# Level products of a chunk: column groups of the array in turn, head by head

## Chip, cores and metric

The kernel runs on one NeuronCore of a Trainium2 chip. The metric is the device time of one execution in microseconds (us): the median over runs. TensorE is PE, with its weight loads shown apart as PEld, VectorE is DVE, ScalarE ACT, GpSimdE POOL; SyncE (SP) issues the transfers.

## What is computed

One layer of a hybrid decoder for a prompt of 1024 tokens and a sample group of 64 tokens: a SwiGLU block, a mixing block, a second SwiGLU block. The mixing block has a windowed attention and, beside it, a gated linear recurrence (HGRN2) with four heads of 128 keys and 128 values. The change touches the recurrence alone. Within a chunk its reference is

```python
G = jnp.cumsum(gb, axis=2)                       # gb = log f
diff = G[:, :, :, None, :] - G[:, :, None, :, :]
decay = jnp.exp(jnp.where(causal, diff, -jnp.inf))
A = jnp.einsum('bhtk,bhsk,bhtsk->bhts', qb, kb, decay)
o = jnp.einsum('bhts,bhsv->bhtv', A, vb) + jnp.einsum('bhtk,bhkv->bhtv', qb * jnp.exp(G), S)
```

with queries `qb`, keys `kb` = 1 - f, and f the forget gate, all float32. `A[t, s]` is a product of a query and a key over 128 key channels, each channel decayed by the gates between s and t.

## The kernel before

**Tokens and stages.** Tokens are worked on in three chunks, n = 0, 1, 2. Chunk 0 has 320 columns (256 prompt tokens and the 64 sample tokens), chunks 1 and 2 have 384 (`WIDTH`, line 26). In blocks of 128 tokens that is two for chunk 0 and three each for the others (`NPB`). The activations lie transposed: channels on the partitions, tokens along the free dimension. For each chunk the combined projection (`w_in_units`, line 1096) makes z; from it come the gates `f`, the queries `Q` and the keys `K`, each a tile of 128 x 4 x width, the 4 being the heads.

**The level products.** `intra` (line 1258) builds A for all blocks of a chunk. It doesn't form the decays pair by pair: it goes through levels h = 1, 2, 4, ..., 64. At level h the tokens are split into pieces of 2h; for a query in the second half of a piece and a key in its first half, the decay is that of the query since the middle times that of the key up to the middle. After each level Q's second halves and K's first halves are multiplied by the gate products `D` of that level (lines 1324 on DVE and 1326 on POOL), so at the next level they hold the decay over a longer stretch. The next level's products need both.

For h up to 16 one call of `blocks` (line 1270) makes all products of a level: for every 32 tokens, number i, and every head a, a matmul with 32 columns of K as the stationary operand and the same 32 columns of Q as the moving one. The result, 32 x 32, goes to PSUM partitions 32 (i mod 4) to 32 (i mod 4) + 31, at a place along the free dimension given by j = i // 4 and a. An operand's columns decide which 32 columns of the array hold it: a product for partitions 0 to 31 uses column group 0, one for 32 to 63 group 1, and so on; all products use all 128 rows. `blocks` is called once as "ld" for the diagonal (line 1290, masked by L1293) and then for each level as "lv" (line 1302); DVE picks the entries of the level by a mask into `C` (line 1305). Each call for chunk 0 makes 10 x 4 products at the diagonal and h = 1, 2, 4, and 8 x 4 at h = 8, 16, where the sample tokens are left out; each call for chunks 1 and 2 makes 12 x 4. Such a run of products is called a burst below.

For h = 32 and 64 the products are written out in `intra` (lines 1308 to 1316, tile "l"): at h = 32 with 32 columns for partitions 0 to 31 and 64 to 95, at h = 64 with 64 columns for partitions 0 to 63. ACT copies them to A (line 1320).

A float32 product shows in the trace as two records of a weight load and two of a matmul.

**What sets the order.** `intra` is a generator that yields after each level. The main program walks through the large projections and calls `tick` (line 127) every few matmuls; `tick` calls `pace` (line 108), which steps the generators of the queue "hg" so that a chunk is done by its due time (`DUE`). The levels of chunk 0 so lie between matmuls of the projection and of the first SwiGLU block's second product (line 283 to 285, `mm3`: three passes of split operands for one product), those of chunks 1 and 2 between the projections of the following work. A scheduler that works with a model of time then fixes the order on each engine; engines work in order.

**Around it.** `load_w` and `split` (lines 259 to 271) bring weights: a transfer to `raw`, a rounded copy `wsph` or `w` on ACT (line 260), the rest on DVE (line 261). The activations of the first SwiGLU block come back from memory as `ar` (line 971). In the attention, line 1242 ("pv") makes its products in pairs for partitions 0 to 63 and 64 to 127; in the attention of the sample group, line 1451 ("spv") makes four products for the four groups of 32 partitions in turn.

Of the kernel before, what the change touches and what calls it, by code (L numbers as in the profile page):

```python
# [18 lines left out]
P = 128  # L19
# [24 lines left out]
def tile_step(ctx: ExitStack, tc: tile.TileContext, A: dict, O: list):  # L44
# [10 lines left out]
    def uid(s):  # L55
        cnt[0] += 1
        return f"{s}_{cnt[0]}"
# [4 lines left out]
    def axbank(s="ax"):  # L62
        return ps.tile([P, 512], F32, tag="ax", bufs=4, name=uid(s))
# [984 lines left out]
    def mixing(tp, h):  # L1048
# [209 lines left out]
        def intra(n):  # L1258

            z, w, wp = Z[n], WIDTH[n], P * NPB[n]  # L1260
            f, Q = z["f"][:, :, :w], z["hq"][:, :, :w]
            K = tp.tile([P, 4, 384], F32, tag="K", name=uid("K"))[:, :, :w]
            D = tp.tile([P, 1524], F32, tag="D", name=uid("D"))
            C = tp.tile([P, 3, 4, 32], F32, tag="cm", name=uid("cm"))
            parts = [(slice(0, P), slice(0, NPB[n]))] + ([(slice(0, NS), slice(2, 3))] if n == 0 else [])

            def span(h):
                return w if h <= 4 else wp

            def blocks(s, x, y, h):  # L1270
                b4 = axbank(s)[:, :384].rearrange("p (j a t) -> p j a t", j=3, a=4)
                for i in range(span(h) // 32):
                    j, cs, ps_ = i // 4, slice(32 * i, 32 * i + 32), slice(32 * (i % 4), 32 * (i % 4) + 32)
                    for a in range(4):
                        PE.matmul(b4[ps_, j, a], x[:, a, cs], y[:, a, cs], start=True, stop=True)  # L1275
                return b4

            def flat(t, rs, js):
                return t[rs, js].rearrange("p j a t -> p (j a) t")

            S.activation(K, f, AF.Copy, bias=1.0, scale=-1.0)
            Ds, off, h = [f], 0, 1
            while h <= 64:
                nx = span(h) // (2 * h)
                Dv = Ds[-1][:, :, :2 * nx].rearrange("p a (x e) -> p a x e", e=2)
                Ds.append(D[:, off:off + 4 * nx].rearrange("p (a x) -> p a x", a=4))
                G.tensor_tensor(Ds[-1], Dv[:, :, :, 0], Dv[:, :, :, 1], op=ALU.mult)
                off += 4 * nx
                h *= 2
            b4 = blocks("ld", K, Q, 1)  # L1290
            for rs, js in parts:
                c = flat(C, rs, js)
                V.tensor_tensor(c, flat(b4, rs, js),  # L1293
                                ident32[rs].unsqueeze(1).to_broadcast([c.shape[0], c.shape[1], 32]), op=ALU.mult)
            V.tensor_tensor(Q, Q, f, op=ALU.mult)
            yield
            At = z["f"]
            h = 1
            while h <= 64:
                ws = span(h)  # L1300
                if h <= 16:
                    b4 = blocks("lv", K, Q, h)
                    for rs, js in parts[:2 if h <= 4 else 1]:
                        c = flat(C, rs, js)
                        V.copy_predicated(c, lmask[h][rs].unsqueeze(1).to_broadcast([c.shape[0], c.shape[1], 32]),
                                          flat(b4, rs, js))
                else:
                    for j0 in range(0, NPB[n], 64 // h + 1):
                        js = range(j0, min(NPB[n], j0 + 64 // h + 1))
                        b4 = axbank(f"l{h}")[:, :len(js) * 4 * h].rearrange("p (j a t) -> p j a t", j=len(js), a=4)  # L1310
                        for j in js:
                            for c in range(0, P, 2 * h):
                                for a in range(4):
                                    k0 = j * P + c
                                    PE.matmul(b4[c:c + h, j - j0, a], K[:, a, k0:k0 + h], Q[:, a, k0 + h:k0 + 2 * h],
                                              start=True, stop=True)
                        Av = At[:, :, P * j0:P * j0 + P * len(js)].rearrange("p a (j t) -> p j a t", j=len(js))
                        for c in range(0, P, 2 * h):
                            for j in range(len(js)):
                                S.copy(Av[c:c + h, j, :, c + h:c + 2 * h], b4[c:c + h, j])  # L1320
                nx = ws // (2 * h)
                Qv, Kv = [t[:, :, :ws].rearrange("p a (x u) -> p a x u", u=2 * h) for t in (Q, K)]
                Dv = Ds.pop(0)[:, :, :2 * nx].rearrange("p a (x e) -> p a x e", e=2)
                V.tensor_tensor(Qv[:, :, :, h:], Qv[:, :, :, h:], Dv[:, :, :, 0:1].to_broadcast([P, 4, nx, h]),
                                op=ALU.mult)
                G.tensor_tensor(Kv[:, :, :, :h], Kv[:, :, :, :h], Dv[:, :, :, 1:2].to_broadcast([P, 4, nx, h]),
                                op=ALU.mult)
                if h == 1:
                    G.memset(At[:, :, :w], 0.0)
                if h == 4 and n == 0:  # L1330
                    z["Ds"] = Ds[0]
                if h == 16:
                    for i in range(4):
                        r, nj = slice(32 * i, 32 * i + 32), 3 if n == 0 and i < 2 else NPB[n]
                        Av = At[r, :, :384].rearrange("p a (j t) -> p j a t", j=3)
                        for j in range(nj):
                            G.tensor_copy(Av[:, j, :, r], C[r, j])
                h *= 2
                yield
            z["K"], z["D"] = K, Ds[0]  # L1340
# [186 lines left out]
        def ready(kind, n):  # L1527
            if n not in MT:
                MT[n] = new_h(n)
            if kind == "at":  # L1530
                gens = [(attn_block(n, b), 9) for b in range(NPB[n])]
                if n == 0:
                    gens += [(sample_attn(), 17), (kv_out(0), 1)]
                if n == 2:
                    gens.append((kv_out(2), 1))
            else:
                gens = [(intra(n), 8)] + [(hgrn_block(n, b), 3) for b in range(NPB[n])]
                if n == 0:
                    gens.append((sample_hgrn(), 14))
                if n == 2:  # L1540
                    gens.append((state_out(), 1))
            queues[kind] += [[n, g, left] for g, left in gens]
# [59 lines left out]
    h = {}  # L1602
# [195 lines left out]
```

## Time and profile before

| | |
|---|---|
| median of 3 runs | 1988.52 us (1987.66 to 1989.71) |
| the profiled execution's own time | 1992.03 us |
| its span, first to last instruction | 1990.3 us |
| granted TensorE clock, mean | 0.998 |
| matmul records | 13549 |
| moved by DMA | 359.54 MB, mean 181 GB/s |

The profile is that of one execution, 3.5 us above the median of the runs. Its views give: the busy time of each engine, whole or in windows ("724.00:790.00 66.00, 66.00 (x786) ..." is a stretch, its length, then busy time and instructions of each engine); groups of instructions by line; and a timeline in which a row is the start, the length, the engine, the line, and out<-in with the shape and the count of like instructions in sequence. "128*32 128x32" is a matmul that uses 128 rows and 32 columns of the array and has a moving operand of 128 x 32. A matmul's own length holds its way through the array, so matmuls in a row overlap; what counts is the time from start to start.

### The profile page before, as it was taken

What the parts mean: (1) busy time and instruction counts of PE and PEld (TensorE: products, weight loads), DVE (VectorE), ACT (ScalarE), POOL (GpSimd) and SP (SyncE); (2) the same over time, 40 slices, a digit from 0 to 9 for tenths busy, and PEclk for the clock granted to TensorE, in tenths of its full rate; (3) what the DMA queues carried; (4) which work ended last, traced back from release to release, by engine and by line L of the source; (5) the groups of instructions that cost most, each with busy time, mean ns of one, the idle gap of its engine ahead of it and who ended that gap; (6) DMA issues with size and microseconds to landing.
All of it is one profiled execution on the core that took longest, in us unless ns stands there. A gap on an engine that the chain in (4) does not pass through costs nothing.

```text
span 1990.3 us, 34623 instructions
## 1 busy us (share of the span) xinstructions
PE 1972.9 (99%) x13549; PEld 1854.7 (93%) x13549; DVE 1371.5 (69%) x1935; ACT 945.3 (47%) x1668; POOL 565.5 (28%) x477
## 2 busy tenths in 40 slices
PE   9999999999999999999999999999999999999998
PEld 8999999999998988888999998999999999999887
DVE  5876656876557657876567666745898888655666
ACT  5733333444445444644345555655544444444453
POOL 0014323655113102111132224101155564510202
PEclk9999999999999999999999999999999999999999
DMA  8544344656777645675444343556465555567874
GB/s 243 168 149 142 136 172 157 201 190 215 228 241 219 180 127 164 219 213 148 118 107 145 96 124 97 173 165 201 151 201 200 190 194 189 209 233 233 287 260 143
DMA packets 372987, 359.54 MB, mean 181 GB/s; under 512 B 41598, under 2 KB 295369, under 8 KB 372809
## 3 DMA queue, kind: packets, MB, share of 16 engines
q1 hardware_dynamic: 370969, 355.37, 56.4%
q8 instruction: 106, 1.74, 0.4%
q10 hardware_dynamic: 1856, 1.97, 0.3%
q14 instruction: 56, 0.46, 0.1%
HBM read 279.33 MB, written 78.94 MB: 180 GB/s over the span
## 4 chain that ended last, share of the span: by engine, by line
PE 91%; DMA 4%; DVE 2%; issue 1%; ACT 1%; SPq 0%; POOL 0%; DVEq 0%; POOLq 0%; ACTq 0%
PE mm L283 27%; PE mm L285 27%; PE mm L284 26%; DMA raw<-in_ffn_w_gu_dram 2%; PE lv L1275 1%; PE c L283 1%; PE c L285 1%; PE c L284 1%; DMA ar<-fa 1%; PE sc L1201 1%; PE pv L1242 1%; PE pT L1227 1%; PE tr L503 1%; DVE w L261 0%; DVE t L750 0%
## 5 line engine op out<-in xcount | busy, mean ns | idle before, releaser
L283 PE MATMUL mm<-h,wsph 128*128 128x320 f32 (+1 forms) x1296 | 416.0, 322 | 0.7 <-ACT wsph L611 0.7
L285 PE MATMUL mm<-h,wspl 128*128 128x320 f32 (+1 forms) x1296 | 409.2, 316 | 1.7 <-DVE wspl L261 1.5
L284 PE MATMUL mm<-h,wsph 128*128 128x320 f32 (+1 forms) x1296 | 409.3, 316 | 0.0
L261 DVE TENSOR_TENSOR wspl<-raw,wsph 128x1024 fp32r<-128x1024 f32 x200 | 250.8, 1256 | 156.3 <-ACT wsph L260 152.9
L260 ACT CAST wsph<-raw 128x1024 fp32r<-128x1024 f32 x200 | 209.2, 1047 | 302.8 <-PE mm L284 230.7
L261 DVE TENSOR_TENSOR w<-raw,w 128x512 fp32r<-128x512 f32 (+1 forms) x226 | 243.5, 1080 | 85.1 <-ACT w L260 83.3
L260 ACT CAST w<-raw 128x512 fp32r<-128x512 f32 (+1 forms) x226 | 169.5, 754 | 258.6 <-PE mm L284 120.6
L283 PEld LDWEIGHTS mm<-h,wsph 128*128 128x128 f32 x1296 | 243.2, 188 | 7.9 <-issue 4.5
L285 PEld LDWEIGHTS mm<-h,wspl 128*128 128x128 f32 x1296 | 243.2, 188 | 3.7 <-DVE wspl L261 1.8
L284 PEld LDWEIGHTS mm<-h,wsph 128*128 128x128 f32 x1296 | 243.5, 188 | 1.1 <-issue 0.8
L283 PE MATMUL mm<-h,w 128*128 128x384 f32 x704 | 236.5, 336 | 2.3 <-DVE big L804 2.2
L284 PE MATMUL mm<-h,w 128*128 128x384 f32 x704 | 236.3, 336 | 0.0
L285 PE MATMUL mm<-h,w 128*128 128x384 f32 x704 | 230.8, 335 | 0.0
L788 POOL TENSOR_TENSOR big<-big 128x384 f32<-128x384 f32 x88 | 110.2, 1252 | 276.8 <-ACT big L801 165.7
L283 PE MATMUL mm<-w,h 128*128 128x512 f32 x462 | 181.3, 395 | 0.0
L284 PE MATMUL mm<-w,h 128*128 128x512 f32 x462 | 180.3, 391 | 0.0
L285 PE MATMUL mm<-w,h 128*128 128x512 f32 x462 | 179.4, 392 | 0.5 <-DVE h L261 0.5
L254 POOL TENSOR_TENSOR sm<-sm,mhalf 128x3 f32<-128x3 f32 (+4 forms) x37 | 36.5, 988 | 492.8 <-DVE sm L424 108.2
L261 DVE TENSOR_TENSOR w<-t,w 128x512 fp32r<-128x512 f32 x176 | 162.4, 935 | 13.3 <-ACT w L260 13.2
L283 PEld LDWEIGHTS mm<-h,w 128*128 128x128 f32 x704 | 132.7, 189 | 2.9 <-DVE big L804 2.9
L284 PEld LDWEIGHTS mm<-h,w 128*128 128x128 f32 x704 | 132.7, 189 | 0.0
L285 PEld LDWEIGHTS mm<-h,w 128*128 128x128 f32 x704 | 132.1, 188 | 0.0
(361 smaller groups left out, 4012.8 us busy)
## 6 DMA issues: line engine op xcount, KB each, us to landing
raw<-in_ffn_w_gu_dram SPq DMA_DIRECT2D x154, 512.0 KB
raw<-in_ffn_w_down_dram SPq DMA_DIRECT2D x74, 512.0 KB
raw<-in_w_in_dram SPq DMA_DIRECT2D x54, 512.0 KB
ar<-fa SPq DMA_DIRECT2D x70, 384.0 KB
big<-in_ffn_w_down_dram SPq DMA_DIRECT2D x88, 256.0 KB
fb<-big SPq DMA_DIRECT2D x44, 512.0 KB
raw<-fb SPq DMA_DIRECT2D x40, 512.0 KB
fa<-big SPq DMA_DIRECT2D x22, 768.0 KB
```

The lines of the kernel that those rows point to most:

```text
L254: G.tensor_tensor(y, x, mhalf[:y.shape[0], :y.shape[1]], op=ALU.pow)
L260: S.copy(hi, src)
L261: (lo_eng or V).tensor_tensor(lo, src, hi.bitcast(F32), op=ALU.subtract)
L283: PE.matmul(out, a[0], b[0], start=first, stop=False, skip_group_check=resume)
L284: PE.matmul(out, a[0], b[1], start=False, stop=False, skip_group_check=resume)
L285: return PE.matmul(out, a[1], b[0], start=False, stop=last, skip_group_check=resume)
L503: PE.transpose(bank[:, i * P:(i + 1) * P], y[kh][:, i, k * P:(k + 1) * P], ident)
L788: G.tensor_tensor(e[:, i], e[:, i], e[:, i + 1], op=ALU.mult)
L1201: PE.matmul(banks[g][:, i * 256:i * 256 + wk], zq[64 * g:64 * g + 64, 2 * pr + i, b * P:(b + 1) * P], kx[64 * g:64 * g + 64, k0:k0 + wk], ...
L1227: PE.transpose(bank[:, (i * nk + kb) * P:(i * nk + kb + 1) * P], pt[g][:, i, kb * P:(kb + 1) * P], ident)
L1242: PE.matmul(ob[q0:q0 + 64, c:c + 64], pT[g][:, k1:k1 + 64], vn[:, vb, g * 64:g * 64 + 64], start=kb == 0, stop=kb == nk - 1)
L1275: PE.matmul(b4[ps_, j, a], x[:, a, cs], y[:, a, cs], start=True, stop=True)
```

## The change

Two loops change places. In `blocks` the loop over the heads is now outside that over the 32-token pieces, and at h = 32 and 64 it is outside that over the pieces of a block. The products, their operands, their places in PSUM and their number are the same.

```diff
             def blocks(s, x, y, h):
                 b4 = axbank(s)[:, :384].rearrange("p (j a t) -> p j a t", j=3, a=4)
-                for i in range(span(h) // 32):
-                    j, cs, ps_ = i // 4, slice(32 * i, 32 * i + 32), slice(32 * (i % 4), 32 * (i % 4) + 32)
-                    for a in range(4):
+                for a in range(4):
+                    for i in range(span(h) // 32):
+                        j, cs, ps_ = i // 4, slice(32 * i, 32 * i + 32), slice(32 * (i % 4), 32 * (i % 4) + 32)
                         PE.matmul(b4[ps_, j, a], x[:, a, cs], y[:, a, cs], start=True, stop=True)
                 return b4
...
                         for j in js:
-                            for c in range(0, P, 2 * h):
-                                for a in range(4):
+                            for a in range(4):
+                                for c in range(0, P, 2 * h):
                                     k0 = j * P + c
                                     PE.matmul(b4[c:c + h, j - j0, a], K[:, a, k0:k0 + h], Q[:, a, k0 + h:k0 + 2 * h],
                                               start=True, stop=True)
```

In a burst the products' column groups were 0 0 0 0 1 1 1 1 2 2 2 2 3 3 3 3 0 0 0 0 ...; now they are 0 1 2 3 0 1 2 3 ... for one head after the other. In chunk 0, where a head has ten products, a head ends with groups 0 and 1 and the next begins with 0. At h = 32 the groups were 0 0 0 0 2 2 2 2 and are 0 2 0 2 0 2 0 2; at h = 64 only the first half of the columns is used and the order is the same as before.

Products of one burst stand as one row in the list of the order, so this doesn't show there. What the scheduler makes of it around the bursts does. On PE, in the last product of chunk 0's projection (`mm_7192`; `lv_7205` is the first level, h = 1, `K_7092` and `big_6733` are K and Q), the burst now stands here:

```order
 L285 MATMUL mm_7192<-h_6042,wspl_7189 128x320
 L283 MATMUL mm_7192<-h_6043,wsph_7188 128x320
+L1275 MATMUL lv_7205<-big_6733,K_7092 32x32 x40
 L284 MATMUL mm_7192<-h_6045,wsph_7188 128x320
 L285 MATMUL mm_7192<-h_6043,wspl_7189 128x320
```

and no longer here, a little further on in the same product:

```order
 L284 MATMUL mm_7192<-h_6045,wsph_7188 128x320
 L285 MATMUL mm_7192<-h_6043,wspl_7189 128x320
-L1275 MATMUL lv_7205<-big_6733,K_7092 32x32 x40
 L283 MATMUL mm_7192<-h_6043,wsph_7188 128x320
 L284 MATMUL mm_7192<-h_6045,wsph_7188 128x320
```

Eight matmuls of the projection that preceded this burst now follow it.

On DVE, at the same time in chunk 0, the diagonal's masking (L1293), the scaling of Q by f (L1295, `big_6733`) and a weight split (L261, `w_7276`, weights of the first SwiGLU block's second product):

```order
 L1175 SCALAR_TENSOR_TENSOR t_982_7179<-t_982_7179,sm_7181,aon 128x512
-L261 TENSOR_TENSOR w_7276<-raw_7273,w_7275 128x1024
 L1293 TENSOR_TENSOR cm_7094<-ld_7103,ident_92 128x256
 L1293 TENSOR_TENSOR cm_7094<-ld_7103,ident_92 64x128
 L1295 TENSOR_TENSOR big_6733<-big_6733,big_6579 128x4x320
+L261 TENSOR_TENSOR w_7276<-raw_7273,w_7275 128x1024
```

The split went from ahead of the three to behind them. Apart from these, three small statistics matmuls (L335) stand behind one matmul that they preceded; ACT, POOL and SP have the order that they had.

## Prediction

> **What bounds the kernel now.** I read the page's totals first, then the three stretches in which the changed products stand, then those products one burst at a time.
>
> ```profile
> PE 1972.9 (99%) x13549; PEld 1854.7 (93%) x13549; DVE 1371.5 (69%) x1935; ACT 945.3 (47%) x1668; POOL 565.5 (28%) x477
> PE 91%; DMA 4%; DVE 2%; issue 1%; ACT 1%; SPq 0%; POOL 0%; DVEq 0%; POOLq 0%; ACTq 0%
> ```
>
> PE is busy for 99% of the span and makes 91% of the chain that ended last. An average says little about one stage, so here are the stretches that hold the level products of the three token chunks (chunk 0: 320 tokens, chunks 1 and 2: 384).
>
> ```profile
> core 0: us, PE busy (x) PEld busy (x) DVE busy (x) ACT busy (x) POOL busy (x), PEclk, DMA share, GB/s
> 724.00:790.00 66.00, 66.00 (x786) 55.96 (x785) 47.23 (x65) 31.29 (x51) 17.27 (x19) 1.00 0.50 149
> 969.00:1056.00 87.00, 87.00 (x1147) 83.28 (x1147) 59.24 (x93) 35.19 (x69) 24.59 (x25) 1.00 0.41 113
> 1162.00:1232.00 70.00, 70.00 (x992) 60.21 (x991) 46.54 (x68) 30.58 (x60) 24.80 (x25) 1.00 0.36 106
> ```
>
> In all three PE is busy for the whole window, at full granted clock, while DVE is busy for 66 to 72% and the DMA engines for 36 to 50%. What PE saves here has nothing waiting beside it yet, so it goes to the end unless a new wait appears.
>
> **What the changed products cost now.** The views of lines 1275 and 1315, then one burst of each size from the timeline (start, length, count):
>
> ```profile
> L1275 PE MATMUL lv<-big,K x1328: 196/196/217, 733.1 to 1208.8; 128*32 128x32 f32 x190
> L1275 PE MATMUL ld<-big,K x272: 196/196/218, 724.6 to 1164.7; 128*32 128x32 f32 x136
> L1315 PE MATMUL l<-big,K x192: 196/196/270, 775.7 to 1229.5; 128*32 128x32 f32 x128, 128*64 128x64 f32 x64
> ```
>
> ```profile
> 743.67 1.82 PE L1275 MATMUL lv<-big,K 128*32 128x32 f32 x80
> 760.24 1.51 PE L1275 MATMUL lv<-big,K 128*32 128x32 f32 x64
> 1002.63 2.12 PE L1275 MATMUL lv<-big,K 128*32 128x32 f32 x96
> 775.67 0.90 PE L1315 MATMUL l<-big,K 128*32 128x32 f32 x32
> 1040.74 1.21 PE L1315 MATMUL l<-big,K 128*32 128x32 f32 x48
> 785.89 1.10 PE L1315 MATMUL l<-big,K 128*64 128x64 f32 x16
> ```
>
> One f32 product shows as two passes (40 products are 80 records), each a load and a matmul. By the code there are 4 bursts of 80 passes, 2 of 64 and 12 of 96 (320 + 128 + 1152 = 1600 = 1328 + 272), and at h=32 one burst of 32 passes and two of 48. Less the last pass's own 0.196, a burst takes from first to last start 1.62 (80), 1.31 (64), 1.92 (96), 0.70 (32) and 1.01 (48) us. That is 0.020 us a pass. At h=64 every product lies in one column group, before and after: no change there, and a useful yardstick: (1.10 - 0.22) / 15 = 0.058 us a pass of 64 by 64.
>
> Now the pace inside one column group: the last three passes of a burst, and a burst that the schedule cut after its first two.
>
> ```profile
> 971.12 0.26 PE L1275 MATMUL ld<-big,K 128*32 128x32 f32 x3
> 1215.04 0.25 PE L1315 MATMUL l<-big,K 128*32 128x32 f32 x2
> ```
>
> (0.26 - 0.196) / 2 = 0.032 us between passes of one group, and 0.25 - 0.196 = 0.054 from the first to the second, where nothing hides the load. The burst's mean of 0.020 is below 0.032: neighbouring groups overlap already where one ends and the next begins, but only there.
>
> **What rotating groups do.** Two places of this kernel already take column groups in turn, the sample group's spv (four groups of 32 columns, the same 128*32 form, 64 moving) and pv (two groups of 64):
>
> ```profile
> L1451 PE MATMUL spv<-kv,t x32: 219/231/243, 864.8 to 928.1; 128*32 128x64 f32 x32
> 864.83 0.26 PE L1451 MATMUL spv<-kv,t 128*32 128x64 f32 x4
> 864.83 0.32 PE L1451 MATMUL spv<-kv,t 128*32 128x64 f32 x8
> L1242 PE MATMUL pv<-vn,t x480: 222/222/271, 694.6 to 1306.3; 128*64 128x64 f32 x160
> 1205.80 1.15 PE L1242 MATMUL pv<-vn,t 128*64 128x64 f32 x32
> ```
>
> Four passes of spv take 0.26 us together where one takes about 0.23: their starts are some 0.01 apart. All eight take 0.32, so the four second passes also run side by side. pv is the longer proof: (1.15 - 0.222) / 31 = 0.030 a pass over 32 passes, half the 0.058 of the same shape in one group. With two groups in turn each group keeps its own pace and the two run at once. I carry that to four groups at 0.032 each, 0.008 a pass overall. It is an extrapolation: no burst here runs four groups for more than two rounds.
>
> The Trainium skill speaks against this (TensorE: Matmul & The Clock Gate, Part 3, on what overlaps): a weight load overlaps matmuls in flight only where the row groups differ. All products here use all 128 rows, so by that rule the order would change nothing and the sum would be 0. The trace does not bear it out: passes of one group follow at 0.032, not at the 0.054 of a load and a pass in line.
>
> **The sum.** A burst lasts as long as its fullest group: with r passes there, 0.054 + (r - 2) x 0.032 + 0.02 for the offset of the others. 96 passes give r = 24 and 0.78 us; 80 also have r = 24 (ten blocks over four groups: three, three, two, two) and 0.78; 64 have r = 16 and 0.52; at h=32 two groups share 32 or 48 passes, r = 16 and 24, 0.52 and 0.78. Saved:
> 12 x (1.92 - 0.78) = 13.7; 4 x (1.62 - 0.78) = 3.4; 2 x (1.31 - 0.52) = 1.6; (0.70 - 0.52) + 2 x (1.01 - 0.78) = 0.6. Together 19.3 us.
>
> Bounds: at best the pace in a group falls to half of 0.054, 0.027, which takes 0.11 more off each burst with r = 24 and 0.07 off one with r = 16, 2.2 us in all. At worst PE cannot be fed faster than it is now (second rival).
>
> **What hides behind it.** After a burst DVE scales Q and POOL scales K, and the next burst needs both. The closest pair of bursts, with the work between:
>
> ```profile
> 1200.60 2.12 PE L1275 MATMUL lv<-big,K 128*32 128x32 f32 x96
> 1203.25 2.01 DVE L1324 TENSOR_TENSOR big<-big,D 128x768 f32<-128x768 f32 x1
> 1202.88 1.57 POOL L1326 TENSOR_TENSOR K<-K,D 128x768 f32<-128x768 f32 x1 [6.02 <-PE lv L1275]
> 1206.88 2.12 PE L1275 MATMUL lv<-big,K 128*32 128x32 f32 x96
> ```
>
> Q is ready at 1205.26, 1.6 us before it is used; K sooner. Both are released by the burst's end and so is PE's filler, so a shorter burst leaves that margin as it is. In chunk 0 the schedule also shifts two things: DVE does L1293 and L1295 ahead of a weight split, and the first lv burst stands eight matmuls earlier.
>
> ```profile
> 727.53 0.61 DVE L1293 TENSOR_TENSOR cm<-ld,ident 128x256 f32<-128x256 f32 x2
> 728.06 1.47 DVE L1295 TENSOR_TENSOR big<-big,big 128x1280 f32<-128x1280 f32 x1
> 732.71 0.31 PE L284 MATMUL mm<-h,wsph 128*128 128x320 f32 x1
> 732.86 0.31 PE L285 MATMUL mm<-h,wspl 128*128 128x320 f32 x1
> 733.10 1.82 PE L1275 MATMUL lv<-big,K 128*32 128x32 f32 x80
> 735.39 0.39 PE L283 MATMUL mm<-w,h 128*128 128x512 f32 x1
> ```
>
> The burst's Q (L1295) is done at 729.53, with 3.6 us to spare. In the new order L1295 comes a split earlier and the burst about 0.84 + 8 x 0.15 = 2.0 us earlier (matmuls there start 0.15 apart): still a margin. The split, over when L1293 began, is put back by these two, about 2 us, and feeds products from 735.39 on. Both cost nothing; without cover the second would cost 2 us once.
>
> **The rivals.**
> 1. *Forecast, 62%.* All 19.3 us arrive. Profiled execution 1992.03 - 19.3 = 1972.7; the median of the runs is 3.5 below that execution, so 1988.52 - 19.3 = 1969.2.
> 2. *PE is fed too slowly, 20%.* The sequencer runs ahead of the array by little:
>
> ```profile
> L1275 PEldq EVENT_SEMAPHORE  x12: 51/51/51, 730.4 to 1206.2; - x12
> ```
>
> The last of these waits ran at 1206.2, before the burst of 1206.88, when pv still had about (1206.73 - 1206.2) / 0.030 = 18 passes to start. So 18 passes stand ready and the rest must be supplied during the burst. The trace proves a supply of one per 0.020 us and no more; at exactly that, each of the 18 large bursts saves 18 x 0.020 = 0.37, 6.6 in all, and with the 0.6 of h=32 7.2: 1981.3. A supply between gives a time between. For: nothing here runs faster for long. Against: the present pace is explained by the groups alone.
> The Trainium skill has a floor of this kind (TensorE: Matmul & The Clock Gate, "Wait — 56ns, not 53.3ns?"): starts never come closer than about 25 ns. Per pass the rows above refute it; per product it would cost 1.2, 1.0 and 0.8 us a burst, an estimate of 12.7 saved and 1975.8.
> 3. *Another engine takes part back, 8%.* The chain runs beside PE from 774.96 to a wait of PE in chunk 0's aftermath:
>
> ```profile
> 774.96 4.47 DMA ar<-fa
> 831.21 0.88 DVE h L261
> 832.14 0.50 PE L285 MATMUL mm<-w,h 128*128 128x512 f32 x1 [0.45 <-DVE h L261]
> ACT w L260 <- PE mm L284: 16.6, 9, 4.4
> ```
>
> If that line of DMA, ACT and DVE work does not move up when PE does, PE waits longer at 832.14 and the first stretch's gain (3.4 + 1.6 + 0.2 = 5.2) is lost: 1974.4. Against it the last row: the casts in that line themselves wait for PE to free buffers.
> 4. *No change, 5%.* Loads wait for all matmuls in flight when the group changes at every product: 1988.5. Against: pv and spv.
> 5. *Slower, 5%.* PE starts passes strictly in order. Each product's second pass must wait 0.054 for its first in the same group, and with the group changing at once nothing runs ahead of it; a product then costs 0.054 + 0.01 = 0.064 where it costs 0.040 now, and any price above 0.040 makes the kernel slower. Bursts of 3.07, 2.56 and 2.05 (48, 40, 32 products): 12 x 1.15 + 4 x 0.94 + 2 x 0.74, and at h=32 0.32 + 2 x 0.53, 20.4 us more: 2008.9. For: now the group holds for eight passes, so this is untested at N=32. Against: eight spv passes in 0.32 us.
>
> **How the numbers follow.** Rivals 1 to 3 are faster by far more than 0.2% (about 4 us, what a measurement of this kernel can tell from no change): 90%. Rival 4 is within it, 5%; rival 5 slower, 5%. The range takes rivals 1 to 3: up to 1981.3, and down to 1969.2 - 2.2 and 1 us of spread between runs, 1966. The likeliest single time is 1969.2.
>
> **What would show it.** In the profile after: bursts of 96 passes near 0.98 us (0.78 + 0.196) in place of 2.12, 80 near 0.98, 64 near 0.72, 48 near 0.98; h=64 bursts unchanged; PE still busy throughout the three stretches, each shorter by 5 to 7 us; the rest of the kernel the same length. Bursts of 96 near 1.8 mean rival 2, bursts as long as now rival 4, near 3.2 rival 5. Short bursts with new PE idle time behind them mean rival 3. I am wrong at the root if bursts shorten and the span does not.

## The result, and the profile after

| | before | after |
|---|---|---|
| median of the runs beside it | 1988.9 us (4 runs, 1987.66 to 1989.71) | 1973.99 us (4 runs, 1973.38 to 1977.14) |
| ratio | | 0.9929, 95% interval 0.9912 to 0.9946 |
| profiled execution, own time / span | 1992.03 / 1990.3 us | 1973.55 / 1971.8 us |

The kernel is 14.9 us faster. A second set of runs (e9 below) gave 0.9930 (0.9918 to 0.9943). The page's totals after, beside those of before:

```profile
PE 1952.9 (99%) x13549; PEld 1833.4 (93%) x13549; DVE 1367.0 (69%) x1935; ACT 944.6 (48%) x1668; POOL 567.1 (29%) x477
PE 91%; DMA 4%; DVE 3%; ACT 1%; issue 1%; SPq 0%; POOL 0%; DVEq 0%; POOLq 0%; ACTq 0%
```

The same instructions with 20 us less of PE, which is still the bound. In the three stretches of the level products, drawn a little closer, nothing waits:

```profile
core 0: us, PE busy (x) PEld busy (x) DVE busy (x) ACT busy (x) POOL busy (x), PEclk, DMA share, GB/s
723.00:784.00 61.00, 61.00 (x785) 50.89 (x785) 43.57 (x64) 30.69 (x50) 16.32 (x19) 1.00 0.52 153
967.00:1047.00 80.00, 80.00 (x1145) 76.28 (x1145) 59.06 (x97) 35.19 (x69) 25.11 (x24) 1.00 0.43 117
1154.00:1217.00 63.00, 63.00 (x991) 53.12 (x990) 45.13 (x66) 30.45 (x59) 23.98 (x24) 1.00 0.39 117
```

The bursts, one of each size, from the timeline:

```profile
741.03 0.95 PE L1275 MATMUL lv<-big,K 128*32 128x32 f32 x80
755.89 0.76 PE L1275 MATMUL lv<-big,K 128*32 128x32 f32 x64
997.94 1.03 PE L1275 MATMUL lv<-big,K 128*32 128x32 f32 x96
769.89 0.70 PE L1315 MATMUL l<-big,K 128*32 128x32 f32 x32
1032.78 0.95 PE L1315 MATMUL l<-big,K 128*32 128x32 f32 x48
779.90 1.10 PE L1315 MATMUL l<-big,K 128*64 128x64 f32 x16
```

Less the last pass's 0.196 that is 0.75, 0.56, 0.83, 0.50 and 0.75 us from first to last start, where it was 1.62, 1.31, 1.92, 0.70 and 1.01; h=64 is as it was. One of the twelve bursts of 96, chunk 1's first, takes 0.06 more (1.09 in the rows below). The burst of 48 in chunk 2 is cut in two before and after alike and gains 0.20. Summed: 11 x 1.09 + 1.03 + 4 x 0.87 + 2 x 0.75 + 0.20 + 0.26 + 0.20 = 18.7 us of PE. Why then 14.9?

The answer comes from following the same matmuls through both traces. Before, the first bursts of the three chunks and chunk 2's last:

```profile
724.55 1.82 PE L1275 MATMUL ld<-big,K 128*32 128x32 f32 x80
969.25 2.13 PE L1275 MATMUL ld<-big,K 128*32 128x32 f32 x96
1162.81 2.13 PE L1275 MATMUL ld<-big,K 128*32 128x32 f32 x96
1228.14 1.61 PE L1315 MATMUL l<-big,K 128*64 128x64 f32 x24
```

After:

```profile
723.65 0.95 PE L1275 MATMUL ld<-big,K 128*32 128x32 f32 x80
967.80 1.09 PE L1275 MATMUL ld<-big,K 128*32 128x32 f32 x96
1154.59 1.03 PE L1275 MATMUL ld<-big,K 128*32 128x32 f32 x96
1213.28 1.61 PE L1315 MATMUL l<-big,K 128*64 128x64 f32 x24
```

The trace after is ahead by 0.90 before any touched instruction, by chance of the start. At chunk 0's last level (785.89 before, 779.90 after) it is ahead by 5.99: 5.1 gained. At chunk 1's first burst only by 1.45: 4.5 of the 5.1 are gone again. Then 8.22 and 14.86: chunks 1 and 2 bring 6.8 and 6.6, all kept. So the touched stretches give 0.6 + 6.8 + 6.6 = 14.0 us, and 0.8 more comes soon behind, where a wait of PE for DVE before pT goes: 14.7, close to the 14.9 of the medians. The spans differ by 18.5 because the profiled execution of before happened to be long elsewhere: 0.9 at the start, and 2.9 near 1450 (1433 after), where PE waited 2.2 us for line 804 and after 0.9. Right behind that longer wait the granted clock was halved for 3.4 us, which makes the other 1.6 (PEclk 0.50 in the row); the trace after has 1.00 there.

```profile
1451.00:1454.00 3.00, 3.00 (x11) 3.00 (x11) 3.00 (x6) 0.00 (x0) 0.14 (x1) 0.50 1.13 299
```

The other kernels below show neither that long a wait nor the halved clock at this place.

Where did chunk 0's gain go? PE's waits between its last level and the next projection, first before, then after:

```profile
PE kT L1371 <- DVE h L465: 1.0, 1, 1.0
PE mm L285 <- DVE h L261: 0.5, 1, 0.5
```

```profile
PE kT L1371 <- DVE h L465: 1.7, 1, 1.7
PE mm L283 <- DVE big L984: 1.5, 2, 1.1
PE mm L283 <- ACT w L260: 0.7, 1, 0.7
PE mm L285 <- DVE h L261: 0.5, 1, 0.5
PE tr L460 <- DVE big L452: 0.4, 1, 0.4
```

1.5 us of waits became 4.8; from one start to the next each new gap costs 0.2 to 0.3 more than the idle time shown, which makes up the rest of the 4.5. PE arrives early and finds DVE and ACT not ready. What they wait for themselves is in ACT's waits in that stretch, three rows of before, then the same three of after (`wsph` and `w` are weights):

```profile
ACT h L260 <- DMA ar<-fa: 9.1, 6, 3.4
ACT wsph L260 <- PE mm L284: 8.8, 6, 3.8
ACT w L260 <- PE mm L284: 4.4, 3, 1.9
```

```profile
ACT h L260 <- DMA ar<-fa: 10.1, 6, 3.4
ACT wsph L260 <- PE mm L284: 5.0, 5, 1.6
ACT w L260 <- PE mm L284: 2.6, 2, 1.4
```

ACT waits 5.6 us less for PE and not less for the reloaded activations. The chain of waits after has that line of work, too:

```profile
771.14 5.27 DMA ar<-fa
829.81 0.88 DVE h L261
```

Its first transfer starts 3.8 us earlier than before (774.96), where PE is already 5.8 ahead, and its last split only 1.4 earlier (831.21), of which 0.9 is the start's chance. The line has its own length, and PE catches up with it.

### The profile page after: what moved, and what is told of

Same layout as the page of the kernel before. It is cut to its first block, busy times and chain, and to the rows that moved or that the text cites. A ratio compares the mean times of both kernels' runs of the same rounds, so it can differ in the third digit from the quotient of the medians.

```text
span 1971.8 us, 34623 instructions
## 1 busy us (share of the span) xinstructions
PE 1952.9 (99%) x13549; PEld 1833.4 (93%) x13549; DVE 1367.0 (69%) x1935; ACT 944.6 (48%) x1668; POOL 567.1 (29%) x477
## 4 chain that ended last, share of the span: by engine, by line
PE 91%; DMA 4%; DVE 3%; ACT 1%; issue 1%; SPq 0%; POOL 0%; DVEq 0%; POOLq 0%; ACTq 0%
PE mm L283 27%; PE mm L285 27%; PE mm L284 27%; DMA ar<-fa 1%; DMA raw<-in_ffn_w_gu_dram 1%; PE c L283 1%; PE c L285 1%; PE c L284 1%; DVE w L261 1%; PE sc L1201 1%; PE pv L1242 1%; PE lv L1275 1%; PE pT L1227 1%; PE tr L503 1%; DVE t L750 0%
## 5 line engine op out<-in xcount | busy, mean ns | idle before, releaser
L261 DVE TENSOR_TENSOR wspl<-raw,wsph 128x1024 fp32r<-128x1024 f32 x200 | 253.0, 1267 | 152.4 <-ACT wsph L260 146.8
L261 DVE TENSOR_TENSOR w<-raw,w 128x512 fp32r<-128x512 f32 (+1 forms) x226 | 243.3, 1080 | 83.6 <-ACT w L260 82.0
L261 DVE TENSOR_TENSOR w<-t,w 128x512 fp32r<-128x512 f32 x176 | 162.0, 933 | 14.8 <-ACT w L260 14.8
```

The costliest lines, as they stand in the source:

```text
L261: (lo_eng or V).tensor_tensor(lo, src, hi.bitcast(F32), op=ALU.subtract)
```

## The experiments

The theory at this point: column groups in turn run at once, and bursts shrink as their fullest group says; a rate of passes sets a floor a little above that; the gain of chunks 1 and 2 arrives, chunk 0's is taken by the line behind it. Times are compared with the kernel before on the same chip, by ratios.

**e1 and e2: chunk 0 alone, chunks 1 and 2 alone.**

```diff
-                for a in range(4):
-                    for i in range(span(h) // 32):
+                for a, i in (ROTATING if n == 0 else OLD):      # e1; e2: the other way round, h = 32 alike
```

(Shown against the change and shortened: ROTATING and OLD stand for the written-out lists of the two orders.)

> Column groups in turn in chunk 0 alone; chunks 1 and 2 as before. Its six bursts and the one at h=32 shorten PE's work by 4 x 0.87 + 2 x 0.75 + 0.2 = 5.2 us. Theory (the line of transfers, ACT and DVE work behind chunk 0 does not move up, so PE waits there): the kernel gains 0.5 to 1.5 us, 1987.4 to 1988.4. Rival (everything that PE saves arrives, and the 4 us between the 18.7 saved in bursts and the 14.9 of the medians is spread between runs): 1983 to 1985.

> Column groups in turn in chunks 1 and 2 alone; chunk 0 as before. PE's bursts shorten by 12 x 1.09 + 0.45 = 13.5 us. Theory: all of it arrives, as nearly all of the gain of the full change, 1974 to 1976. Rival (losses are spread over all three chunks in proportion, 14.9 of 18.7): 13.5 x 0.8 = 10.8, 1978.

e1: 1987.24 us against 1989.41, ratio 0.9989 (0.9980 to 0.9998), a gain of 0.4 to 4.0 us, 2.2 by the medians. That excludes the whole 5.2 us of the rival and reaches only the low end of its range (3.9, from 1988.9 to 1985); the median lies over the theory's 0.5 to 1.5. In its trace, by the positions of the matmuls, chunk 0 gains 5.1 us and keeps 1.4 of them, where the full change keeps 0.6. PE's waits behind chunk 0 in e1:

```profile
PE kT L1371 <- DVE h L465: 1.7, 1, 1.7
PE mm L283 <- DVE big L984: 1.5, 2, 1.1
PE mm L285 <- DVE h L261: 0.5, 1, 0.5
PE tr L460 <- DVE big L452: 0.2, 1, 0.2
```

The same waits as in the full change but for that on ACT's w, with chunks 1 and 2 untouched: they belong to chunk 0's gain. e2: 1977.6 us, ratio 0.9935 (0.9922 to 0.9949), 10.1 to 15.5 us. The interval holds both theory and rival, and the median is nearer the rival; its runs spread from 1973.64 to 1981.02. The times do not decide. The trace, of an execution that took 1974.52, is as the theory has it, and nothing shows what the longer executions lost. In it PE's waits behind chunk 0 are

```profile
PE kT L1371 <- DVE h L465: 0.8, 1, 0.8
PE mm L283 <- ACT h L260: 0.3, 1, 0.3
```

and from the end of chunk 0's aftermath to the matmuls behind chunk 2 its matmuls gain 13.8 us on those of before, as the full change does with 14.2.

**e3 and e5: fewer groups in turn.** How far does the number of groups set the burst?

```diff
-                for a in range(4):
-                    for i in range(span(h) // 32):
+                for a, i in [(a, i) for g in (0, 2) for a in range(4)
+                             for i in range(span(h) // 32) if i % 4 in (g, g + 1)]:      # e3
+                for a, i in [(a, i) for g in range(4) for i in range(g, span(h) // 32, 4)
+                             for a in range(4)]:                                          # e5, h = 32 as before
```

> Column groups 0 and 1 in turn through all heads, then 2 and 3. Theory (as many passes run at once as there are groups in turn, each group at 0.032 us a pass): a burst of 96 takes two times 24 rounds, 1.45 to 1.53 us from first to last start, 0.4 to 0.48 less than before; chunks 1 and 2 gain 5 to 6 us, chunk 0's gain of some 1.5 is mostly lost: 1982 to 1984. Rival (any alternation does it, because what counts is only that a product's second pass does not wait behind its first): bursts as with four groups, 1974.

> The other end: all products of column group 0, then all of group 1, 2, 3; h=32 as before. Theory (each group at 0.032 us a pass, overlap only where the group changes; each of the eleven seams of a burst of 96 saves 8 x 0.032 - 0.154 = 0.10, and now there are three): bursts of 96 take 2.77 us from first to last start, of 80 2.26, of 64 1.75; chunks 1 and 2 lose 10.1 us, chunk 0 3.4, of which PE's waits behind chunk 0 take up to 1.5: 2000 to 2004. Rival (the old pace of 0.020 a pass was what PE can be fed, in any order): no change, 1988 to 1990.

A burst of 96 in e3, then one of each size in e5:

```profile
1000.71 1.62 PE L1275 MATMUL lv<-big,K 128*32 128x32 f32 x96
```

```profile
1007.59 2.92 PE L1275 MATMUL lv<-big,K 128*32 128x32 f32 x96
743.79 2.42 PE L1275 MATMUL lv<-big,K 128*32 128x32 f32 x80
761.55 1.91 PE L1275 MATMUL lv<-big,K 128*32 128x32 f32 x64
```

With two groups 1.62 - 0.20 = 1.42, just under the 1.45 to 1.53 expected; with one, from first to last start, 2.73, 2.22 and 1.72 where 2.77, 2.26 and 1.75 were expected; with the old order 1.92, with four groups 0.83. Ratios: e3 0.9964 (0.9952 to 0.9977), 1981.72 against 1989.41, 0.3 under the range expected (a gain of 7.7 by the medians); e5 1.0064 (1.0049 to 1.0079), 2000.58 against 1987.68. Both rivals fall: two groups are not as good as four, and the old 0.020 a pass, which the change goes below and e5 above, was no rate of supply.

**e6: is 0.0084 us a pass a rate of its own?** With four groups the burst of 96 took 0.83 and not the 0.78 of its groups. Its last fifty passes:

```profile
998.36 0.61 PE L1275 MATMUL lv<-big,K 128*32 128x32 f32 x50
```

(0.61 - 0.196) / 49 = 0.0084, where a quarter of 0.032 is 0.0080. e6 doubles the passes without adding columns to move:

```diff
-                        PE.matmul(b4[ps_, j, a], x[:, a, cs], y[:, a, cs], start=True, stop=True)
+                        for u in (0, 16):
+                            PE.matmul(b4[ps_, j, a, u:u + 16], x[:, a, cs], y[:, a, 32 * i + u:32 * i + u + 16],
+                                      start=True, stop=True)
```

> The full change with each product issued as two of 16 moving columns: the same results, twice the passes. Theory (once some 36 passes that stood ready are gone, passes come at 0.0085 us, which is the feed): a burst of 192 passes takes 1.5 to 1.7 us from first to last start, 0.7 to 0.85 more than with the full change; 1983 to 1986. Rival (0.0085 is still the groups' own pace; a pass of 16 costs 0.013 + 0.005 in its group): 48 x 0.019 = 0.9 us a burst, 1974 to 1976.

```profile
999.01 2.02 PE L1276 MATMUL lv<-big,K 128*32 128x16 f32 x192
1000.01 0.77 PE L1276 MATMUL lv<-big,K 128*32 128x16 f32 x65
1213.45 1.69 PE L1276 MATMUL lv<-big,K 128*32 128x16 f32 x157
1217.40 0.62 PE L1276 MATMUL lv<-big,K 128*32 128x16 f32 x35 [2.25 <-issue]
PE lv L1276 <- issue: 5.5, 3, 2.7
```

An undisturbed burst takes 2.02 - 0.18 = 1.84, twice the rival's 0.9 and more than the theory's 1.5 to 1.7; in its middle a pass comes every (0.77 - 0.18) / 64 = 0.0092. Half the columns, no quicker pass. But e6 doesn't separate its two sides. The rival took 0.018 us for a pass of 16 columns in its own group, and the trace shows no such pace. These are the last two passes of a burst, where by the order only the last product's group has passes left:

```profile
724.25 0.21 PE L1276 MATMUL ld<-big,K 128*32 128x16 f32 x2
```

They start 0.21 - 0.18 = 0.03 apart, as those of 32 columns do. At 0.032 the groups alone would take 0.054 + 46 x 0.032 + 0.02 = 1.55 for 48 passes each; only the 0.3 above that speaks for something more.

Better evidence for a common limit lies in the change's own bursts. In the one of 96 at 997.94 the fifth and the 33rd pass start 0.22 us apart, 0.0079 a pass, and only behind them comes the 0.0084. The burst of 80, whose groups are unequal so that it needs a pass every 0.0096 on average, took 0.75, no longer than its fullest group was said to need (0.78). A limit for passes in all near 0.0084 fits this; it was not tested alone, and whether the sequencer or the array would set it stays open.

Neither side expected the rows at 1213.45 and 1217.40 and the one of waits for "issue": some bursts broke off for up to 2.7 us in which PE waited for nothing that the profile shows. So the kernel took 1998.88 us (ratio 1.0055, 1.0041 to 1.0069), far above both forecasts: in its trace the undisturbed length of the 18 bursts makes 17 us more than in the change's, their stops 7.

**e4, e7, e10: the line behind chunk 0.** If ACT's casts of the reloaded activations hold up the weight casts behind them, moving these splits to POOL gives part of chunk 0's gain back:

```diff
-                split(t[:, :n, 1], t[:, :n, 0], raw[:, :n])
+                if inner:
+                    split(t[:, :n, 1], t[:, :n, 0], raw[:, :n])
+                else:
+                    G.tensor_copy(t[:, :n, 1], raw[:, :n])
+                    G.tensor_tensor(t[:, :n, 0], raw[:, :n], t[:, :n, 1].bitcast(F32), op=ALU.subtract)
```

> The full change, and the split of the reloaded activations (ar, second product of the first feed-forward block, in its last stretch) moved from ACT and DVE to POOL, so that ACT's weight casts no longer stand behind casts that wait for a transfer. Theory (ACT's and DVE's order is what holds the line after chunk 0): PE's waits between chunk 0's last level and chunk 1's projection go from 4.7 us to under 2, 1969.5 to 1972. Rival (the one transfer in flight at a time, or POOL's own slower split, sets the pace): 1974 or more.

> The old order of the products with the split of the reloaded activations on POOL as in e4. Theory (that split matters only where PE has run ahead): PE waited 1.5 us behind chunk 0 before, so at most that is gained, 1987.9 to 1989.4. Rival (it is a gain of its own, whatever the order of the products): 2.6 us as between e4 and the full change, 1986.8 or less.

> The full change itself, beside the next two on one chip. Theory: the same kernel as before takes 14 to 15 us more (14.7 by the positions of the matmuls in the two traces, without what differs outside the touched stretches).

> e4 again. Theory: 2.5 to 3 us below the full change, what PE's waits behind chunk 0 give back. Rival (e4's gain was a difference between chips): within 1 us of it.

e4: ratio 0.9908 (0.9895 to 0.9922), 1971.42 against 1989.41. Its waits behind chunk 0, then those of the same kernel in e10:

```profile
PE kT L1375 <- DVE h L465: 1.1, 1, 1.1
PE tr L460 <- DVE h L465: 0.6, 1, 0.6
```

```profile
PE kT L1375 <- DVE h L465: 1.3, 1, 1.3
PE tr L460 <- DVE K L1376: 1.3, 1, 1.3
PE tr L460 <- DVE h L465: 0.6, 1, 0.6
```

The waits for ACT and for line 984 are gone; 1.7 to 3.2 us remain of 4.8. By the positions of the matmuls 3.4 and 2.7 us of chunk 0's gain are kept where the full change keeps 0.6 and, in e9, 1.1. On one chip e9 took 1974.36 and e10 1973.05 (ratios 0.9930 and 0.9924, their intervals overlap), so by time the 2.5 to 3 us expected were not seen; 1.3 was, between theory and rival. (e9 is 14.1 us under the kernel before by the medians, in the 14 to 15 expected.) Nor are the two traces alike: e4's ran at a granted clock of 0.50 from 824.9 to 828.3, in the middle of this stretch, e10's at 1.00 throughout, so e10's 3.2 is the fairer remainder. e7, the same split with the old order of products: 1989.39 against 1987.68, ratio 1.0011 (1.0002 to 1.0019). It is no gain of its own, and not the small gain that the theory allowed: it costs a little where PE had not run ahead. The line is shown as the place of the loss. What holds it there is shown in part only: ACT's and DVE's work there, but not that alone. The move also takes the splits' work off both engines, so it doesn't tell their order from their load.

**e8 and e11: two groups at h=64 as well.**

```diff
-                                    PE.matmul(b4[c:c + h, j - j0, a], K[:, a, k0:k0 + h], Q[:, a, k0 + h:k0 + 2 * h],
+                                    r0 = 64 * (a % 2) if h == 64 else c
+                                    PE.matmul(b4[r0:r0 + h, j - j0, a], K[:, a, k0:k0 + h], Q[:, a, k0 + h:k0 + 2 * h],
...
+                                    for e in range(2):
+                                        S.copy(Av[:h, j, e::2, h:], b4[h * e:h * e + h, j, e::2])
```

> e4, and at h=64 the odd heads' products go to partitions 64 to 127, so that two column groups of 64 take turns there; ACT brings them back in twice as many copies of half the size. Theory: the bursts at h=64 fall from 1.39 to 0.75 us in chunks 1 and 2 and from 0.88 to 0.46 in chunk 0, 1.3 to 1.7 us in all: 1969.5 to 1970.5. Rival (the additional ACT copies delay weight casts by as much): no change from e4, 1971 to 1972.

> e8 again. Theory: 1.5 to 2 us below e10, as its bursts at h=64 are shorter by 0.46 + 2 x 0.69. Rival (the additional copies on ACT give it back): within 1 us of e10.

```profile
1039.26 0.92 PE L1320 MATMUL l<-big,K 128*64 128x64 f32 x24
```

The burst falls from 1.39 to 0.70, all three together by 1.9 us. The operands are the same and only the partitions of the results differ, so it is these that decide the column group of a product. e8: 1970.55 against 1987.68, ratio 0.9916 (0.9902 to 0.9929): in the range expected, but on another chip than e4, and by ratio no gain on e4's 0.9908. e11, beside e9 and e10: 1971.35, ratio 0.9912 (0.9899 to 0.9926), 1.7 below e10's median as the theory has it, but with overlapping intervals. Of the kernels tried this is the fastest by its median on that chip, 3.0 us under the change alone; the intervals of that pair also touch, so it is likely better, not shown to be.

## Why the prediction was right, and where it was not

The time lay in the range, and the direction and its mechanism held; the single time, 1969.2, was 4.8 too low.

- **PE bounds the stretches, and rotating groups run at once.** Shown: e5, e3 and the change scale with the number of groups in turn, and the pace inside a group of 0.032 carried over, the extrapolation from pv and spv included.
- **The sum of 19.3.** PE's bursts gave 18.7. The term of the bursts of 96 was mis-sized, 0.78 for 0.83, and that of 64, 0.52 for 0.56, likely by a limit near 0.0084 us a pass; those of 80 and at h=32 came out 0.02 to 0.03 better than said.
- **The second rival.** If there is a floor for passes, it lies near 0.0084 and not at 0.020; it costs 0.05 in a burst of 96 or 64 and nothing in one of 80. The pace changes behind 33 passes, where the prediction had 18 standing ready. e5 shows that the old 0.020 was the groups' overlap.
- **The step that failed: "All 19.3 us arrive".** It rested on PE being busy through the three windows, with nothing waiting beside it. That was so inside them, and after as well. The loss lies behind the first, where PE had waited only 1.5 us before. The runs showed there that 4.5 of chunk 0's 5.1 us go, the third rival's place. Its time, 1974.4, is close to the 1973.99 measured partly by luck: it took 5.2 us for the loss, and it has neither the 0.6 us that the bursts fell short nor the 0.8 us gained behind chunk 2, which nobody forecast. It had 8%, because casts in that line waited for PE to free buffers. The 16.6 us of such waits that it rested on were those of 724 to 1232; in the line's own stretch ACT waited 13.2 us for PE and also 9.1 for the transfers, and the latter stay when PE comes earlier.
- **What hides behind it.** Right: no new wait for Q, K or the shifted split shows inside the stretches.
- **Fourth and fifth rival.** Neither: bursts shrank as four groups at once say, so loads do overlap matmuls that use the same rows: each pass has a load of its own, and passes start 0.0084 us apart where a load and a pass in line took 0.054.

## What to carry to other kernels

Small products that use different column groups should be issued with the groups in turn from one to the next; a burst then lasts about as long as its fullest group (the fastest here took 0.0088 us a pass over its length), and the trace shows both paces beforehand if any code already alternates. A window in which the bound engine never waits proves that time saved there leaves the window, not that it reaches the end: look behind it for a place where that engine waits even a little, and at what the engines it waits for are themselves waiting for. A run's median and one profiled execution can differ by several us; following the same instruction through two traces tells which part of a difference belongs to the change.

## What the runs showed of the hardware beyond that

Passes on four column groups start as close as 0.0084 us on average over fifty passes, each with its own load. Passes of 16 moving columns came no faster than those of 32, in their own group either. Behind waits of PE of 2.2 us (before, near 1450) and stops of 2.2 and 2.7 us (e6) the granted clock was 0.50 for 3.4 us; in e4 it was so near 825 behind a wait of 1.1 us.

And in bursts of 160 and 192 such passes PE stood still now and then, for up to 2.7 us, without a wait that the profile can name. Counted through the trace's records of PE (loads, matmuls and semaphore waits, by start), the five stops of 0.3 us and more stand at records 9921, 13761, 14273, 20673 and 21185: their distances, 3840, 512, 6400 and 512, are all multiples of 256. That points to instructions being supplied in blocks of 256, and to bursts so dense that a block sometimes comes late; no run tried it. The 0.06 us in chunk 1's first burst of the change does not stand at such a place (record 12696), and its cause is open.
